# Alternating the layers of two token groups, with the norms and the sample group moved inside the stages and the weights packed on the host

## The chip, the cores and the metric

The kernel runs on all 8 cores of one Trainium2 chip (two dies of four cores). Every core does the same work on its own data. The metric is the device time of the slowest core, in microseconds (us), taken as the median of several runs. Some runs here fall in a slower state, in which some cores show a lower granted TensorE clock; such runs are named as slow and are left out of every comparison.

The engines are PE (TensorE, matrix products), ACT (ScalarE), DVE (VectorE), POOL (GpSimd) and SP (SyncE, which here only issues transfers). The lines of the profile use these names.

## The reference

The reference is one step of a two-layer trunk for a prompt (8 sequences of 2048 tokens, 1024 features, one sequence for each core) and for 128 sample rows (16 for each core). One layer is:

```python
h = rmsnorm(x, norm_g)                                  # over 1024 features
a_in, a_gate, u, v, b_gate = split(h @ w_in)            # w_in 1024 x 2560: five blocks of 512
# A: trailing means over 2, 4, 8, 16 positions (one window per 128 channels), minus the token
a_out = (pooled(a_in) @ w_pool) * pool_scale * silu(a_gate)
# B: chunks of 128 positions, 4 heads
b_out = u * (tril(w_s) @ rmsnorm(v) + b_s) * silu(b_gate)
x = x + concat(a_out, b_out) @ w_out                    # w_out 1024 x 1024
```

A sample row is one new token, so its trailing means also need up to 15 earlier rows of `a_in`, which come in as a state (`st`, two layers x 16 rows x 15 x 512). A final RMSNorm ends both paths. The weights arrive in float32 and are multiplied in bfloat16.

## The kernel before

The prompt is cut into four groups of 512 tokens. I call one group's pass through one layer a **stage**: norm, transposes, five projection blocks (V, A, two gates, U), pooling, chunk product, output projection, residual add. There are eight stages. The kernel before takes them group by group, (0,0), (0,1), (1,0) and so on, written as (group, layer):

```python
WIN_ORDER = (C_V, C_AIN, C_AGATE, C_BGATE, C_U)
for l in range(2):
    for cb in WIN_ORDER:                     # POOL's queue casts float32 to bfloat16 on the way
        wlist.append((win[l][:, :, cb:cb + 512],
                      win_d[l][:, cb:cb + 512].rearrange("(k p) e -> p k e", p=128), f"win{l}_{cb}"))
    # [cut: wpool and two halves of w_out]
issue_weights(100)                           # all of them at the start

for G in range(NG):                          # [cut: arguments and hooks]
    layer_group(G, 0, ...)                   # the second layer's norms run at the end of this stage
    layer_group(G, 1, ...)                   # the next group's norms run at the end of this one
fin_b = finals_batched(NG - 1, split=True)
sample_rest(1, mid_hook=fin_b)               # the sample group's second layer: at the very end
sample_final()
```

The sample group runs beside and after the last prompt stage, with 16 of the 128 rows of a matmul's output in use.

All work is emitted into one list for each engine and runs there **in that order**.

Of the kernel before, what the change touches and what calls it, by code (L numbers as in the profile page):

```python
# [28 lines left out]
NT = SEQ // 128  # L29
NHB = 3  # L30
HALO = 16
AW = HALO + GT
C_AIN, C_AGATE, C_U, C_V, C_BGATE = 0, 512, 1024, 1536, 2048
WINDOWS = (2, 4, 8, 16)

# [8 lines left out]

class Buf:
    __slots__ = ("name", "writer", "readers")

    def __init__(self, name):
        self.name = name
        self.writer = None  # L50
        self.readers = []

class Op:
    __slots__ = ("eng", "fn", "deps", "dma", "tok", "used", "group")

    def __init__(self, eng, fn, dma=None, group=False):
        self.eng = eng
        self.fn = fn
        self.deps = []
        self.dma = dma  # L60
        self.group = group
        self.tok = None
        self.used = False

class Sched:
    def __init__(self):
        self.ops = {e: [] for e in ENGS}
        self.all = []

    def emit(self, eng, fn, reads=(), writes=(), deps=(), dma=None, group=False):  # L70
        op = Op(eng, fn, dma, group)
# [3 lines left out]
        for b in reads:  # L75
            if b.writer is not None:
                dd.append(b.writer)
        for b in writes:
            dd.extend(b.readers)
            if b.writer is not None:  # L80
                dd.append(b.writer)
        dd.extend(d for d in deps if d is not None)
# [11 lines left out]
        for b in writes:  # L94
            b.writer = op
            b.readers = []
        self.ops[eng].append(op)
        self.all.append(op)
        return op

    def resolve(self):
        keys = {}
        dma_cnt = {}
        group_ops = {}
        for e in ENGS:
            cnt = 0
            for op in self.ops[e]:
                if op.dma is not None:
                    dma_cnt[op.dma] = dma_cnt.get(op.dma, 0) + 16
                    op.tok = (op.dma, dma_cnt[op.dma])  # L110
                    keys[op.dma] = None
                    if op.group:
                        group_ops.setdefault(op.dma, []).append(op)
                elif op.used:
                    cnt += 1
                    op.tok = (e, cnt)
                    keys[e] = None
        for k, ops in group_ops.items():
            for op in ops:
                op.tok = (k, dma_cnt[k])  # L120
        return keys

    def run_engine(self, e, h, sems):
        waited = {}
        for op in self.ops[e]:
            for d in op.deps:
                key, val = d.tok
                if waited.get(key, 0) < val:
                    h.wait_ge(sems[key], val)
                    waited[key] = val  # L130
# [5 lines left out]

class Banks:
    def __init__(self, tensors, tag):
        self.t = tensors
        self.bufs = [Buf(f"{tag}{i}") for i in range(len(tensors))]  # L140
        self.nxt = 0

    def alloc(self):
        i = self.nxt
        self.nxt = (self.nxt + 1) % len(self.t)
        return self.t[i], self.bufs[i]

def build_program():
# [12 lines left out]
    ng_d = din("norm_g", [2, D])  # L161
    win_d = din("w_in", [2, D, DIN])
    wpool_d = din("w_pool", [2, 4, 128, 128])
    psc_d = din("pool_scale", [2, WA])
    vng_d = din("v_norm_g", [2, WB])
    ws_d = din("w_s", [2, 4, 128, 128])
    bs_d = din("b_s", [2, 4, 128])
    wout_d = din("w_out", [2, D, D])
    fng_d = din("fng", [1, D])
    cid_d = din("c_ident", [128, 128])  # L170
    ctril_d = din("c_tril", [128, 128])
    cinv_d = din("c_invcnt", [1, 64])
    csel_d = din("c_sel", [120, 128])
    cm01_d = din("c_m01", [2, 2])
    gT_d = din("gT_h", [128, 16])
    pscT_d = din("pscT_h", [128, 8])
    ws00_d = din("ws00_h", [1, 8])
    bs0_d = din("bs0_h", [1, 8])
# [3 lines left out]
    pp_d = dout("pp", [2, PB, WA])  # L182
# [4 lines left out]
    with ExitStack() as es:  # L187
# [3 lines left out]
        def ps(name, shape, dt):  # L191
            return es.enter_context(nc.psum_tensor(name, list(shape), dt))

        win = [sb(f"win{l}", [128, 8, DIN], BF16) for l in range(2)]
        wout = [sb(f"wout{l}", [128, 8, D], BF16) for l in range(2)]
# [5 lines left out]
        a_sb = sb("a_sb", [128, 2, AW], F32)  # L201
        halo = sb("halo", [128, 2, 4, HALO], F32)
        Tt = sb("Tt", [128, 2, AW], F32)
        d_sb = sb("d_sb", [128, 4, GT], BF16)
        sg = sb("sg", [128, 4, GT], BF16)
        mix = sb("mix", [128, 8, GT], BF16)
        vn_sb = sb("vn_sb", [128, TPG, WB], BF16)
        vscr = sb("vscr", [128, WB], F32)
        junk = vscr[:, :].bitcast(BF16)
        vnf = sb("vnf", [128, WB], F32)  # L210
        pp_sb_ = vnf
        pp_sb = pp_sb_
        g_bc = sb("g_bc", [128, D], F32)
        gT = sb("gT", [128, 2, 8], F32)
        vg_bc = sb("vg_bc", [128, 2, WB], F32)
        psc = sb("psc", [128, 2, 4, 1], F32)
        ident = sb("ident", [128, 128], BF16)
        identf = xg[:, 5, 512:640]
        tril = xg[:, 5, 640:768]
        wsm = xg[:, 5, 768:1024].bitcast(BF16).rearrange("p (h j) -> p h j", h=4)  # L220
        invcnt = sb("invcnt", [128, 4, 16], F32)
        fix_t = sb("fix_t", [128, 16], F32)
        nhalf = sb("nhalf", [128, 4], F32)
        epsb = sb("epsb", [128, 1], F32)
        ones2 = sb("ones2", [2, 128], BF16)
        fl = lambda ap: ap.rearrange("p a b -> p (a b)")
        r3 = lambda ap: ap.rearrange("p (h i) -> p h i", h=4)
        bsf_l = [r3(xg[0:2, 4, 0:512]), r3(xg[0:2, 4, 512:1024])]
        bhif = r3(Tt[0:2, 0, 0:512])
        bhi = r3(hb[0:2, 2, 0:512])  # L230
        blo = r3(hb[0:2, 2, 512:1024])
        bias2 = sb("bias2", [2, 2, 4, 128], BF16)
        m01 = sb("m01", [2, 2], F32)
        ssx = sb("ssx", [128, 4 * 2 * SEQ // 128 // 2 + 64], F32)
        rsx = ssx
        ss4 = sb("ss4", [128, 2 * (SEQ // 128) + 4, 4], F32)
        rs4 = ss4
        xs_sb = xg[0:NS, 0, :]
        hbs = hb[0:NS, 0, :]
        hTs = sb("hTs", [128, 8, NS], BF16)  # L240
        st_sb = xg[0:120, 1, :].rearrange("p (t c) -> p t c", t=2)
        sel = sb("sel", [120, 2, 4, NS], F32)
        ains = pp_sb_[0:NS, :]
        ds_s = d_sb[0:NS, 0, :]
        dsT = sb("dsT", [128, 4, NS], BF16)
        tmp_s = Tt[0:NS, 0, 0:512]
        sga_s = a_sb[0:NS, 0, 0:512]
        sgb_s = a_sb[0:NS, 1, 0:512]
        s_s = Tt[0:NS, 1, 0:512]
        vns = vnf[0:NS, :]  # L250
        mixs = hb[0:NS, 1, :]
        mixTs = hTs
        psc_bc = vscr[0:NS, :]
        ws00 = sb("ws00", [NS, 2, 4, 1], F32)
        bs0 = sb("bs0", [NS, 2, 4, 1], F32)
# [8 lines left out]
        ALIAS = {  # L264
            "bhif": ["T0"], "bhi": ["hb2"], "blo": ["hb2"], "mixTs": ["hTs"], "pp_sb": ["vnf"],
            "hbs": ["hb0"], "st_sb0": ["x1"], "st_sb1": ["x1"], "ains": ["pp_sb"], "ds_s": ["d0"],
            "tmp_s": ["T0"], "sga_s": ["a_sb0", "a_halo0"], "sgb_s": ["a_sb1", "a_halo1"], "s_s": ["T1"],
            "vns": ["vnf"], "mixs": ["hb1"], "xs": ["x0"], "psc_bc": ["vscr"],
        }

        def buf(name):
            if name in ALIAS:
                return [buf(n) for n in ALIAS[name]]
# [4 lines left out]
        col_ctr = [0]  # L278

        def newcol():  # L280
            c = col_ctr[0]
            col_ctr[0] += 1
            return c
# [3 lines left out]
        def _okey():  # L287
            okey_ctr[0] += 1
            return f"out{okey_ctr[0]}"

        col4_ctr = [0]

        def newcol4():
            c = col4_ctr[0]
            col4_ctr[0] += 1
            return c

        stage_ops = []

        def cdma(out_ap, in_ap, wbuf, eng=SP):  # L300
            return S.emit(eng, lambda h, o=out_ap, i=in_ap: h.dma_start(out=o, in_=i),
                          writes=[wbuf], dma="const", group=True)

        def load_tile(t, deps=()):
            slot = t % NSLOT
            r0 = t * 128
            return S.emit(SP, lambda h, s=slot, r=r0: h.dma_start(out=xg[:, s, :], in_=x_d[r:r + 128, :]),
                          writes=[buf(f"x{slot}")], dma=f"xl{slot}", deps=deps)

        S.emit(SP, lambda h: h.dma_start(out=identf[:, :], in_=cid_d[:, :]), writes=[buf("identf")], dma="cident")  # L310
        for l in range(2):
            S.emit(SP, lambda h, l=l: h.dma_start(out=gT[:, l, :], in_=gT_d[:, l * 8:(l + 1) * 8]),
                   writes=[buf(f"gT{l}")], dma=f"cgT{l}")
        for t in range(4):
            load_tile(t)
        def prep_dma(l):
            stage_ops.append(S.emit(SP, lambda h, l=l: h.dma_start(
                out=bsf_l[l][:, :, :], in_=bs_d[l].rearrange("(o h) i -> o h i", o=1).broadcast_to([2, 4, 128])),
                writes=[buf(f"bsf{l}")], dma=f"bsf{l}"))

        ckey = [0]

        def cdma1(out_ap, in_ap, wbuf):
            ckey[0] += 1
            return S.emit(SP, lambda h, o=out_ap, i=in_ap: h.dma_start(out=o, in_=i), writes=[wbuf], dma=f"c{ckey[0]}")

# [758 lines left out]
```

## Time and profile before

The time before is 592.83 us (median of 3 runs, 591.86 to 595.3). The trace's slowest core spans 592.6 us.

| Part of the span | us | What limits it |
|---|---|---|
| First two of eight stages | 192 | weights arriving, work on DVE; PE busy 127 |
| A pair of stages after that | 116.3 | PE, busy 109.7 |
| After the last prompt matmul | 26 | a serial chain for the 16 sample rows |

The rows are read from the lines below. These lines are from the page of the kernel before: busy time and instructions of PE; then PE's busy share, the granted clock and the DMA engines' busy share in 40 equal slices of 14.8 us (9 is 90% or more); then packets, megabytes and share of the software queue that carries the weights.

```profile
PE 493.6 (83%) x2456; PEld 224.1 (38%) x2456; DVE 332.1 (56%) x748; ACT 175.4 (30%) x278; POOL 110.9 (19%) x158
PE   0259179868699999899999988999999989799993
PEclk9999778979989999999899999998999899988998
DMA  7999999940000000410000005100000021401003
q0 software_dynamic: 15616, 14.94, 18.8%
```

The reader sees three parts. The DMA engines are nearly full in the first eight slices, and PE has holes there. In the middle PE is nearly full. The next lines are from the table of engine busy time for chosen stretches (stretch, its length, busy time and instructions of PE, PEld, DVE, ACT and POOL, then granted clock, DMA share and GB/s).

```profile
0.00:192.00 192.00, 126.84 (x602) 56.91 (x603) 99.26 (x259) 48.71 (x74) 34.53 (x51) 0.91 0.70 110
192.00:308.50 116.50, 109.64 (x561) 50.68 (x560) 69.00 (x143) 40.59 (x64) 24.03 (x34) 0.99 0.10 37
308.50:424.60 116.10, 109.67 (x562) 50.65 (x560) 69.02 (x143) 40.60 (x64) 23.96 (x34) 0.99 0.10 37
```

The first two stages take 192 us. After that a pair of stages takes 116.3 us, of which PE is busy 109.7: PE is the limit. The end is different again. Lines of the timeline of PE (start, length, line and operation, output and inputs, count, and in brackets the idle time before it and what ended it):

```profile
562.25 3.63 PE L702 MATMUL pF<-wout,mix 128*128 128x512 bf16 x16
569.28 7.07 PE L759 MATMUL pF<-win,hTs 128*16 128x512 bf16 x32
580.57 5.30 PE L878 MATMUL pF<-wout,hTs 128*16 128x512 bf16 x16 [0.48 <-DVE hTs L750]
```

L702 is the prompt's last output projection. It is over at about 566 us, and 26 us of sample work follow. The sample's matmuls (`128*16`: 16 output columns of the array in use) cost as much as full ones (`128*128`): 32 in 7.07 us, and the 32 full ones from 191.77 us on took 7.07 us too.

### The profile page before, as it was taken

Reading aid. Unit: us, or ns where it says so; the run is one execution under the profiler, and the core shown is the slowest. Engines: PE = TensorE matmul, PEld = TensorE weight load, DVE = VectorE, ACT = ScalarE, POOL = GpSimd, SP = SyncE. Lnnn points to the kernel's source line nnn. Section 1 sums busy time; section 2 is a strip of 40 time slices with the busy share of each in tenths; the row PEclk is TensorE's granted clock in tenths of the full one; section 3 lists DMA queues with packets and bytes.
Section 4 is the critical chain, followed back from the end, with each engine's and each line's share of the span. In section 5 each row is a group of like instructions: output and inputs, shape, how many; then the busy total and the mean of one; then the engine's idle time right before and its main releaser. Section 6 shows DMA issues by size and latency. Waiting matters only on the chain.

```text
span 592.6 us, 7987 instructions; the slowest of 8 cores (582.6 to 592.6 us)
## 1 busy us (share of the span) xinstructions
PE 493.6 (83%) x2456; PEld 224.1 (38%) x2456; DVE 332.1 (56%) x748; ACT 175.4 (30%) x278; POOL 110.9 (19%) x158
## 2 busy tenths in 40 slices
PE   0259179868699999899999988999999989799993
PEld 0224023423235444344354434444544344334341
DVE  0247674448735664666357655673575456644556
ACT  2501040511223243433233425243234152211230
POOL 9002110113001501241005021501140215100020
PEclk9999778979989999999899999998999899988998
DMA  7999999940000000410000005100000021401003
GB/s 153 180 171 167 152 223 150 156 67 1 1 0 2 0 1 2 177 71 38 1 1 0 2 0 213 48 26 1 1 19 3 0 108 38 120 1 39 1 7 146
DMA packets 24244, 36.86 MB, mean 62 GB/s; under 512 B 3057, under 2 KB 18793, under 8 KB 24171
## 3 DMA queue, kind: packets, MB, share of 16 engines
q0 software_dynamic: 15616, 14.94, 18.8%
q1 hardware_dynamic: 8587, 21.42, 11.0%
q8 instruction: 20, 0.33, 0.2%
q14 instruction: 21, 0.17, 0.1%
HBM read 42.12 MB, written 10.09 MB: 88 GB/s over the span
## 4 chain that ended last, share of the span: by engine, by line
PE 54%; DVE 19%; issue 7%; DMA 6%; ACT 5%; POOL 4%; SPq 1%; another core or an unknown queue 1%; DVEq 1%; POOLq 0%; ACTq 0%
PE pF L506 23%; PE pF L702 16%; PE pF L519 9%; DMA xg<-w_s 4%; DVE win L376 3%; DVE Tt L543 3%; DVE mix L690 2%; DVE vn_sb L581 2%; ACT vscr L454 2%; DVE ss L569 2%; PE pF L759 2%; PE pT L487 2%; PE pF L878 2%; POOL Tt L543 1%; ACT hb L477 1%
## 5 line engine op out<-in xcount | busy, mean ns | idle before, releaser
L506 PE MATMUL pF<-hT,win 128*128 128x512 bf16 x1024 | 233.5, 385 | 10.4 <-ACT a_sb L642 4.6
L506 PEld LDWEIGHTS pF<-hT,win 128*128 128x128 bf16 x1024 | 100.8, 99 | 136.8 <-issue 21.4
L702 PE MATMUL pF<-wout,mix 128*128 128x512 bf16 x512 | 122.8, 397 | 7.3 <-DVE ssx L465 3.1
L702 PEld LDWEIGHTS pF<-wout,mix 128*128 128x128 bf16 x512 | 50.4, 101 | 68.6 <-issue 19.2
L519 PE MATMUL pF<-win,hT 128*128 128x512 bf16 x272 | 65.1, 397 | 10.5 <-DVE win L376 6.8
L468 POOL TENSOR_TENSOR ssx<-ssx,nhalf 128x1 f32<-128x1 f32 (+1 forms) x31 | 20.0, 646 | 227.9 <-DVE ssx L465 227.9
L707 DVE TENSOR_TENSOR xg<-pF,xg 128x512 f32<-128x512 f32 x64 | 44.1, 689 | 32.7 <-PE pF L702 31.3
L454 ACT ACTIVATE vscr<-xg 128x1024 bf16<-128x1024 f32 (+1 forms) x35 | 36.7, 1049 | 85.0 <-DVE xg L707 58.9
L477 ACT ACTIVATE hb<-xg,ssx 128x1024 bf16<-128x1024 f32 x32 | 36.7, 1148 | 60.6 <-POOL ssx L468 59.1
L575 POOL TENSOR_TENSOR ss<-ss,nhalf 128x4 f32<-128x4 f32 x32 | 32.4, 1012 | 106.5 <-DVE ss L573 106.5
L672 DVE TENSOR_TENSOR sg<-pF,sg 128x512 bf16<-128x512 f32 x32 | 22.1, 691 | 49.9 <-PE pF L506 36.3
L487 PE MATMUL pT<-ident,hb 128*128 128x128 bf16 x256 | 21.1, 230 | 31.4 <-ACT hb L477 31.4
L519 PEld LDWEIGHTS pF<-win,hT 128*128 128x128 bf16 x272 | 27.0, 102 | 43.9 <-issue 16.9
L642 ACT COPY a_sb<-pF 128x512 f32<-128x512 f32 x32 | 18.7, 585 | 83.2 <-DVE d_sb L560 32.6
L565 ACT ACTIVATE vscr<-pF 128x512 f32<-128x512 f32 x32 | 19.1, 595 | 81.4 <-PE pF L519 45.5
L552 DVE SCALAR_TENSOR_TENSOR d_sb<-Tt,a_sb 128x512 bf16<-128x512 f32 x32 | 22.1, 691 | 23.0 <-POOL halo L550 22.7
L581 DVE SCALAR_TENSOR_TENSOR vn_sb<-pF,ss,vg_bc 128x128 bf16<-128x128 f32 x120 | 33.8, 344 | 1.0 <-issue 0.4
L668 ACT ACTIVATE sg<-pF 128x512 bf16<-128x512 f32 x32 | 19.1, 597 | 49.1 <-DVE mix L662 25.7
L465 DVE TENSOR_SCALAR ssx<-ssx 128x1 f32<-128x1 f32 (+1 forms) x31 | 4.7, 152 | 50.4 <-ACT vscr L454 50.4
L487 PEld LDWEIGHTS pT<-ident,hb 128*128 128x128 bf16 x256 | 17.4, 103 | 40.5 <-issue 35.8
L491 DVE COPY hT<-pT 128x1024 bf16<-128x1024 bf16 x32 | 21.9, 687 | 17.1 <-PE pT L487 17.1
L543 DVE TENSOR_TENSOR Tt<-Tt 128x512 f32<-128x512 f32 (+3 forms) x40 | 27.9, 697 | 4.5 <-DVE Tt L543 0.5
(90 smaller groups left out, 386.2 us busy)
## 6 DMA issues: line engine op xcount, KB each, us to landing
win<-w_in POOLq DMA_DIRECT2D x10, 1024.0 KB, 67.3
xg<-x SPq DMA_DIRECT2D x16, 512.0 KB, 5.8
y<-xg SPq DMA_DIRECT2D x16, 512.0 KB, 2.9
wout<-w_out POOLq DMA_DIRECT2D x4, 1024.0 KB, 88.7
xg<-st SPq DMA_DIRECT2D x4, 240.0 KB, 2.7
pso<-st SPq DMA_DIRECT2D x2, 448.0 KB, 5.9
vg_bc<-v_norm_g SPq DMA_DIRECT2D x2, 256.0 KB, 18.0
xg<-w_s SPq DMA_DIRECT2D x2, 256.0 KB, 24.7
```

Source lines behind the costliest of these rows:

```text
L454: S.emit(ACT, lambda h: h.activation(out=junk[0:nparts, 0:n_feat], in_=src_ap, func=AF.Square, accum_out=ssx[0:nparts, c:c + 1]), reads=li ...
L477: S.emit(ACT, lambda h: h.activation(out=hb[:, j, :], in_=xa, func=AF.Copy, scale=rsx[:, c:c + 1]), reads=[xbuf(G, i), rb], writes=[buf(f" ...
L487: r = h.transpose(out=pt[:, k * 128:(k + 1) * 128], in_=hb[:, j, k * 128:(k + 1) * 128], identity=ident[:, :])
L506: r = h.matmul(out=pf[:, 0:GT], lhsT=win[l][:, k, col0:col0 + 128], rhs=hT[:, k, :], start=(k == 0), stop=(k == 7))
L519: r = h.matmul(out=pf[:, :], lhsT=hT[:, k, i * 128:(i + 1) * 128], rhs=win[l][:, k, col0:col0 + 512], start=(k == 0), stop=(k == 7))
L543: S.emit(PENG, lambda h, dst=dst, src=src, c0=c_from, sh=shift: h.tensor_tensor(out=dst[:, c0:AW], in0=src[:, c0:AW], in1=src[:, c0 - sh:A ...
L552: S.emit(DVE, lambda h, src=src: h.scalar_tensor_tensor(out=d_sb[:, g, :], in0=src[:, HALO:AW], scalar=1.0 / w, in1=a_sb[:, sl, HALO:AW], ...
L575: S.emit(POOL, lambda h: h.tensor_tensor(out=rs4[:, c, :], in0=rs4[:, c, :], in1=nhalf[:, :], op=ALU.pow), reads=[rb, buf("nhalf")], write ...
L581: r = h.scalar_tensor_tensor(out=o, in0=pf[:, hh * 128:(hh + 1) * 128], scalar=rs4[:, c, hh:hh + 1], in1=vg_bc[:, l, hh * 128:(hh + 1) * 1 ...
L672: S.emit(DVE, lambda h, pf=pf, hh=hh: h.tensor_tensor(out=sg[:, hh, :], in0=pf[:, 0:GT], in1=sg[:, hh, :], op=ALU.mult), reads=[pfb, buf(f ...
L702: r = h.matmul(out=pf[:, :], lhsT=mix[:, k, i * 128:(i + 1) * 128], rhs=wout[l][:, k, hf * 512:(hf + 1) * 512], start=(k == 0), stop=(k == 7))
L707: S.emit(DVE, lambda h, pf=pf, xa=xa, hf=hf: h.tensor_tensor(out=xa[:, hf * 512:(hf + 1) * 512], in0=pf[:, :], in1=xa[:, hf * 512:(hf + 1) ...
```

## The change

Its intent is to give each layer's weights twice as long to arrive (two groups run through layer 0 before layer 1 is needed), to keep PE from waiting between stages, to take work off PE and DVE, and to take the sample group off the end. The core of the diff, with cuts marked:

```diff
-for G in range(NG): layer_group(G, 0, ...); layer_group(G, 1, ...)
+order = [(0, 0), (1, 0), (0, 1), (1, 1), (2, 0), (3, 0), (2, 1), (3, 1)]
+hooks = {
+    (0, 0): {"g0": [prep_ws], "g1": [lambda: load_state(0), lambda: load_state(1)], "b0": [load_w],
+             "b2": [load_w], "u0": [load_w], "u2": [load_w], "o00": [misc_loads],
+             "o11": [lambda: state_sum(0), lambda: state_sum(1)], "o30": [load_w]},
+    (1, 0): {"v2": [load_w], "a0": [load_w]},
+    (2, 0): {"v0": [lambda: sample_layer(0, lambda: None)]},
+    (2, 1): {"v0": [lambda: sample_layer(1, sample_final)]},
+}
 # hooks: "g0" is "after the first unit of the first gate", "b" the second gate,
 # "o11" after the second half of the second tile of the output projection

 # in stage(): the next stage's norms run inside this one
+unit_u(G, l, hh); norm_b(*nxt, hh); norm_c(*nxt, hh)        # [cut: conditions]
+norm_tr(*nxt, 0); norm_tr(*nxt, 1)                          # before the output projection
+# [cut] norm_tr(*nxt, 2) after tile 0 of it, norm_tr(*nxt, 3) after tile 1

 # weights: each block is one contiguous 16 KB row per partition, packed on the host
-win_d[l][:, cb:cb + 512].rearrange("(k p) e -> p k e", p=128)
+win_d = din("win_h", [2, 5, 128, 8 * 512])
 # norm gain: out of the weights, into the eviction of the transposes
-h.tensor_scalar(out=win[l][:, k, cb:cb + 512], ..., scalar1=gT[:, l, k:k + 1], op0=ALU.mult)   # x80
+S.emit(DVE, lambda h: h.tensor_tensor(out=hT[:, :, i * 128:(i + 1) * 128], in0=pt[...],
+    in1=gT(l).unsqueeze(2).broadcast_to([128, 8, 128]), op=ALU.mult), ...)
 # chunk bias: from a matmul into DVE's eviction; wide windows: shifted adds -> one scan [cut]

 # sample group: four column quadrants, output partitions 32j..32j+31
-h.matmul(out=pf[0:NS, :], lhsT=hTs[:, k, :], rhs=win[l][:, k, col0:col0 + 512], ...)
+h.matmul(out=p1_[32 * j:32 * j + 32, :]..., lhsT=hTs[:, k, :],
+         rhs=win[l][:, 0:4, k, j * 128:(j + 1) * 128], ..., tile_position=(0, 32 * j))

 # all on SP's queue, in this order
+gate = [buf(f"win0_{U_}").writer]                           # x of group 1 waits for the U block
+for i in range(TPG): load_x(1, i, deps=gate)
+sdma(qc[:, :], q_d[:, :], writes=[buf("qc")])
+for j in range(4):                                          # four pieces of 16 KB, one buffer
+    sdma(xs[32 * j:32 * j + NS, :], xs_d[:, j * 256:(j + 1) * 256], writes=[buf("xs")], key=f"xs{j}")
+# [cut] pso: state rows to the output; then load_state(0), load_state(1), four pieces each
+def state_sum(l):                                           # DVE: sums of 1, 3, 7, 15 state rows
+    for j in range(4):
+        S.emit(DVE, lambda h, j=j, n=n: h.tensor_reduce(out=ssum[32 * j:32 * j + NS, l, :], ...))
```

## The prediction

> What bounds the kernel now. The per-stretch table of engine busy time splits the slowest core's 592.6 us into three parts.
> (a) Start, 0 to 192 us, for two of the eight stages (4 token groups x 2 layers). The DMA engines are saturated until about 122 us. The timeline shows layer-0 projection blocks landing at about 23 (first), 55 and 61.5 us (last), and the last layer-1 output weights at about 127 us: some 7 us per 2.1 MB block, about 295 GB/s of reads. Added to that: 80 norm-gain multiplications of weights on DVE (21.5 us in the groups), mask and bias preparation, an idle PE at 60 to 74 us (its clock granted falls to 0.5), and in the second stage a wait of pooling and v-norm on each other (PE busy 74% at 140-150, 62% at 150-160).
> (b) Steady state: one group, both layers, takes 116.3 us, PE busy 109.7, clock 0.99; 512-column matmuls start every 0.216 us. PE is the limit; waits and transposes cost about 7 us per pair.
> (c) End: 533 to 592 us, last output projection with the sample group on 16 of 128 rows. Its full-width matmuls are 112 x 0.216 = 24 us, and after the last prompt matmul (566 us) 26 us of serial sample chain follow.
>
> What the change does. Two groups alternate, so layer 0 runs twice (about 54 us more) before layer-1 weights are needed, and the next stage's norms run under the present one's gate and U matmuls; the transposes sit where PE would wait for the mix. The gain moves to the transpose eviction: 80 multiplications go, but 32 evictions grow from 0.69 to about 1.2 us (DVE about +16 us spread out, harmless at about 60% busy). The bias matmul goes: 32 x 0.32 = 10 us of PE. Pooling of wide windows becomes a scan, estimated 1.2 us each instead of 2 to 2.8. Blocks of 16 KB per partition help DMA a little; I estimate 6.5 to 7 us per block.
>
> Sum.
> - Stage 1 follows the weights: first block about 18 us, U about 46, output weights about 70 (x of group 1 competes). Then 12 to 14 us of output projection: stage ends at about 85.
> - Seven stages at (116.3 - 7)/2 - 1.3 = 53.3 us: 373.
> - [...]
> - Remaining bubbles 5; tail (last add, square sum, scale, store) 8.
> Total 483, so 484 us, range 465 to 515. Nearly all of the saving (about 105 start, 25 to 30 steady, most of 26 at the end[...]) is on the critical path, because PE is the limit throughout.
>
> Chances: faster 0.97, same 0.02, slower 0.01.
>
> Right if: stage 2 starts at 75 to 95 us; stages 2 to 8 take 52 to 56 us each with PE idle under 2 us; no PE gap over 5 us after 90 us; tail under 12 us. Wrong if: output weights land after 85 us; a stage takes over 57 us because DVE or POOL (U products wait for a POOL multiplication, 1.04 us each) falls behind; quadrant matmuls run one after another[...].
>
> [...] Before, all eight cores show 0.99 in the steady stretches[...].

The sum came to 483 us. The terms still printed add up to 471 (85, 373, 5 and 8); the missing one, 12 us for the sample group, is cut, and so are the 10 us for serial quadrant matmuls.

## The result

The kernel after takes 521.57 us (median of 4 runs: 520.88, 521.4, 521.74 and one slow run of 533.28; the median of the three fast ones is 521.4), beside 592.52 for the kernel before on the same chip. The ratio is 0.8786 (95% interval 0.8755 to 0.8817). Ratios here are the mean time of one kernel's fast runs over that of the other's in the same rounds, so they are not quite the ratio of the medians. The kernel is 12% faster, and 6.6 us slower than the top of the predicted range.

The page of the kernel after (slices of 13 us), with the same lines as above, and the shares of the chain that ended last, by engine:

```profile
PE 456.0 (88%) x2486; PEld 214.1 (41%) x2486; DVE 284.8 (55%) x484; ACT 168.2 (32%) x276; POOL 156.6 (30%) x224
PE   8795767740699999999999999999999999999994
PEclk9899697785699999999999999999999999999997
DMA  6999999534490000005500350000200000030003
q0 software_dynamic: 2160, 14.94, 17.6%
PE 66%; DMA 21%; DVE 4%; issue 4%; ACT 2%; POOL 1%; SPq 1%; POOLq 0%; DVEq 0%; ACTq 0%
```

From the twelfth slice PE is full to the end. The loss is all in the first eleven slices: one of them is empty (0), and 21% of the last chain is DMA. The packing shows too: the software queue carries the same megabytes in 2160 packets instead of 15616, so a packet is 6.9 KB instead of 957 B (14.94 MB over the count). The steady part, in the table of stretches:

```profile
186.70:239.90 53.20, 52.44 (x278) 24.93 (x277) 33.29 (x61) 21.38 (x34) 17.37 (x26) 1.00 0.03 12
293.00:350.40 57.40, 56.63 (x384) 27.38 (x383) 35.41 (x64) 20.83 (x38) 19.62 (x27) 1.00 0.21 66
```

A plain stage takes 53.2 us with PE idle for 0.8; a stage with the sample group in it takes 57.4. The largest waits of PE (what waited, for what, microseconds, times, longest):

```profile
PE pF L418 <- DVE xg L567: 25.4, 1, 25.4
PE pT L388 <- ACT hb L378: 17.6, 19, 4.0
PE pF L523 <- DMA wpool<-wpool_h: 8.9, 1, 8.9
```

The first is one single wait, and all eight cores have it (22.9 to 26.8 us). PE's V projection of stage 2 needs a PSUM bank that DVE's residual add (L567) has yet to empty. DVE had nothing hard to do. The chain of waits over this stretch, in order of time (start, length, what; cut to the long pieces):

```profile
56.70 44.37 DMA xs_sb<-xs
101.13 1.63 DMA xs_sb<-xs
102.83 1.71 DMA xs_sb<-xs
...
106.32 5.82 DMA win<-st
...
123.36 4.23 DMA wout<-st
...
130.50 3.37 DVE ssum L885
```

This is read from top to bottom as one sentence. The first 16 KB of sample input took 44.37 us to land. That is not the price of 16 KB alone: on SP's queue it stood behind group 1's x (four tiles of 512 KB, the last landed at 92 us) and `qc` (386 KB, landed 43.7 us after its issue at 56.15), 2450 KB in all. The pieces behind it were issued one after the other; then came the state, piece by piece; then DVE could sum it. DVE's own timeline shows where it stood meanwhile:

```profile
119.37 6.17 DVE L885 TENSOR_REDUCE ssum<-win 16x128 f32<-16x128 f32 x4 [20.74 <-DMA win<-st]
127.68 6.17 DVE L885 TENSOR_REDUCE ssum<-wout 16x128 f32<-16x128 f32 x4 [1.74 <-DMA wout<-st]
134.16 2.88 DVE L567 TENSOR_TENSOR xg<-pF,xg 128x512 f32<-128x512 f32 x4
```

DVE sat idle for 20.74 us at the head of its queue, and the four residual adds that PE needed stood behind the sums. They ran in the order of DVE's list, and the price here is 25.4 us.

The second loss is the length of stage 1. The output weights landed at about 72 us (70 predicted), but the output projection ended only at 106. The transposes of group 1 are now part of stage 1, and its x arrived late. ACT's timeline for the last of four tiles:

```profile
92.06 1.06 ACT L354 ACTIVATE hb<-xg 128x1024 bf16<-128x1024 f32 x1 [4.47 <-DMA xg<-x]
```

That tile's x landed at 92 us. PE transposed it at about 96 us, ahead of the last 32 matmuls of the projection (9.6 us), and the stage ended at 106.

The sum can now be set beside the prediction's. All measured numbers are read from the profiled core's trace.

| Term | Predicted, us | Measured, us |
|---|---|---|
| Stage 1 ends | 85 | 106.0 |
| Stages 2 to 8 without sample and without the one long wait | 373 | 372.3 |
| Sample group | 12 | 8.8 (57.4 + 57.6 less twice 53.1) |
| Bubbles; measured: the one long wait | 5 | 25.4 |
| Tail | 8 | 7.5 |
| Sum | 483 | 520.0 |

Two terms are wrong, by 21 and by 20 us. The experiments ask what causes each of them.

### The profile page after: what moved, and what is told of

Same layout as the page of the kernel before. It is cut to its first block, busy times and chain, and to the rows that moved or that the text cites. A ratio compares the mean times of both kernels' runs of the same rounds, so it can differ in the third digit from the quotient of the medians.

```text
span 520.1 us, 7837 instructions; the slowest of 8 cores (509.4 to 520.1 us)
## 1 busy us (share of the span) xinstructions
PE 456.0 (88%) x2486; PEld 214.1 (41%) x2486; DVE 284.8 (55%) x484; ACT 168.2 (32%) x276; POOL 156.6 (30%) x224
## 3 DMA queue, kind: packets, MB, share of 16 engines
q0 software_dynamic: 2160, 14.94, 17.6%
## 4 chain that ended last, share of the span: by engine, by line
PE 66%; DMA 21%; DVE 4%; issue 4%; ACT 2%; POOL 1%; SPq 1%; POOLq 0%; DVEq 0%; ACTq 0%
PE pF L406 37%; PE pF L562 15%; DMA xs_sb<-xs 9%; PE pF L418 9%; DMA win<-win_h 6%; DMA wout<-st 2%; DMA win<-st 2%; DMA xg<-x 2%; ACT hb L378 1%; PE pT L388 1%; PE pF L536 1%; DVE hT L392 1%; PE pF L523 1%; SPq L292 1%; DVE ssum L885 1%
## 5 line engine op out<-in xcount | busy, mean ns | idle before, releaser
L418 PE MATMUL pF<-win,hT 128*128 128x512 bf16 x256 | 59.1, 388 | 25.4 <-DVE xg L567 25.4
L562 PEld LDWEIGHTS pF<-wout,mix 128*128 128x128 bf16 x512 | 50.3, 100 | 59.9 <-issue 7.1
L354 ACT ACTIVATE hb<-xg 128x1024 bf16<-128x1024 f32 x48 | 50.3, 1049 | 60.6 <-DVE xg L567 37.8
L545 POOL TENSOR_TENSOR mix<-vscr,mix 128x512 bf16<-128x512 f32 x32 | 36.4, 1156 | 99.3 <-DVE vscr L541 99.2
L362 POOL TENSOR_TENSOR rsx<-rsx,nhalf 128x1 f32<-128x1 f32 x48 | 26.4, 553 | 122.0 <-DVE rsx L359 122.0
L517 ACT ACTIVATE mix<-pF 128x512 bf16<-128x512 f32 x64 | 38.2, 597 | 76.1 <-PE pF L406 73.5
L434 POOL TENSOR_TENSOR rs<-rs,nhalf 128x4 f32<-128x4 f32 x32 | 35.2, 1101 | 72.2 <-DVE rs L432 72.1
L567 DVE TENSOR_TENSOR xg<-pF,xg 128x512 f32<-128x512 f32 x64 | 44.0, 690 | 21.3 <-PE pF L562 19.2
L378 ACT ACTIVATE hb<-xg,rsx 128x1024 bf16<-128x1024 f32 x32 | 36.1, 1144 | 55.5 <-POOL rsx L362 55.4
L541 DVE SCALAR_TENSOR_TENSOR vscr<-pF,kc,bias 128x512 f32<-128x512 f32 x32 | 23.3, 749 | 45.6 <-PE pF L536 35.3
L392 DVE TENSOR_TENSOR hT<-pT,kc 128x1024 bf16<-128x1024 bf16 x32 | 38.4, 1217 | 2.5 <-PE pT L388 2.4
L501 DVE SCALAR_TENSOR_TENSOR mix<-Tt,a_sb 128x512 bf16<-128x512 f32 x32 | 22.2, 693 | 24.3 <-POOL halo L493 21.5
L429 DVE TENSOR_REDUCE ss<-vscr 128x4 f32<-128x512 f32 x32 | 21.9, 683 | 13.5 <-ACT vscr L425 13.2
```

The costliest lines, as they stand in the source:

```text
L354: S.emit(ACT, lambda h: h.activation(out=junk, in_=src, func=AF.Square, accum_out=ssx[:, c:c + 1]), reads=[srcb], writes=[junkb, buf(f"ssx ...
L362: S.emit(POOL, lambda h: h.tensor_tensor(out=rsx[:, c:c + 1], in0=rsx[:, c:c + 1], in1=nhalf[:, 0:1], op=ALU.pow), reads=[buf(f"rsx{c}"), ...
L378: S.emit(ACT, lambda h: h.activation(out=hb[:, j, :], in_=xap(G, i), func=AF.Copy, scale=rsx[:, c:c + 1]), reads=[xbuf(G, i), buf(f"rsx{c} ...
L392: S.emit(DVE, lambda h: h.tensor_tensor(out=hT[:, :, i * 128:(i + 1) * 128], in0=pt[:, :].rearrange("p (k t) -> p k t", k=8), in1=gT(l).un ...
L418: r = h.matmul(out=pf[:, :], lhsT=hT[:, k, i * 128:(i + 1) * 128], rhs=win[l][:, V_, k, :], start=(k == 0), stop=(k == 7))
L434: S.emit(POOL, lambda h: h.tensor_tensor(out=rs4[:, c, :], in0=rs4[:, c, :], in1=nhalf[:, :], op=ALU.pow), reads=[rb, buf("nhalf")], write ...
```

## The experiments

Fourteen kernels ran, and all gave correct results. The letters in the expectations name theories. A: DVE is held by the state sums. C: the layer-1 weights, issued in stage 1 though nothing needs them before stage 3, crowd out x, the sample input and the state. E: the long packets of the packed weights crowd out the small transfers. G: only the order and the chaining on SP's queue delay the state. I, J, L and P belong to single later runs and are explained there. Times are medians; ratios are against the kernel before in the same rounds.

### Four single edits of the kernel after

**e1_sum_late.** The sums move to stage 2. The layer-1 loads whose space the state uses move behind them.

```diff
 (0, 0): ... "o00": [misc_loads],
-        "o11": [lambda: state_sum(0), lambda: state_sum(1)], "o30": [load_w]},
-(1, 0): {"v2": [load_w], "a0": [load_w]},
+(1, 0): {"a3": [lambda: state_sum(0)], "b0": [lambda: state_sum(1)], "u2": [load_w], "o00": [load_w], "o30": [load_w]},
```

> Edit: the two sums of the sample state on DVE (12.3 us of work plus the wait for their loads) move from the output projection of stage 1 into stage 2 (behind the last pooling unit and the first B gate unit); the last three layer-1 weight loads follow them; no transfer of stage 1 moves. Theory A (the 25.4 us PE gap at 109.6 us is DVE held in program order by a sum whose input lands at 119 us): the gap shrinks to under 6 us and the kernel takes 495 to 502 us. Rival B (PE would have waited there anyway, for weights or for x of group 1): the gap stays over 15 us and the time stays above 512 us.

Measured: 499.38 us (498.56 to 500.02), ratio 0.8422 (0.8392 to 0.8452). The wait of 25.4 us is gone from PE's list, whose largest single waits are now:

```profile
PE pF L523 <- DMA wpool<-wpool_h: 8.2, 1, 8.2
PE pF L523 <- DVE mix L501: 4.9, 1, 4.9
```

The state's pieces landed hardly earlier (SP's chain of them ran from 104.7 to 120.6 us); only DVE no longer stood waiting for them. This shows theory A. Of the wait's 25.4 us the kernel gained 22.2. The 12.3 us of summing now stand in stage 2, which takes 59.9 us on the profiled core; PE's 4.9 us are a wait for an instruction of DVE that stands right behind the first sum.

**e2_l1_late.** The order on DVE stays as it was, but all layer-1 weights are issued in stage 2.

```diff
-(0, 0): ... "b0": [load_w], "b2": [load_w], "u0": [load_w], "u2": [load_w], ... "o30": [load_w]
-(1, 0): {"v2": [load_w], "a0": [load_w]},
+(1, 0): {"v0": [load_w], "v1": [load_w], "v2": [load_w], "v3": [load_w], "a0": [load_w], "a1": [load_w], "a2": [load_w]},
```

> Edit: the layer-1 weight loads, four of which are issued during stage 1, are all issued in stage 2; nothing else moves. Theory C (transfers on the SP queue are slow because layer-1 weights, not needed before 187 us, share the DMA engines): x of group 1 lands by about 74 us instead of 92, the sample rows within 25 us of issue instead of 44, the state by 90 us; stage 1 ends about 10 us earlier and the gap falls to about 5 us: 487 to 497 us. Rival D (the SP queue is slow by itself, by its chain of waits or by layer-0 weights alone): x lands within 4 us of before, and the time changes by under 8 us.

Measured: 496.67 us (496.5 to 497.17), ratio 0.8376. Group 1's x had landed by about 75 us instead of 92 (its second tile at 72), and the first piece of sample input took 18.6 us instead of 44.4. Stage 2 started at 92.15 us on the profiled core instead of 105.97. The wait on DVE shrank but did not vanish (expected about 5 us, measured 14.1). A line of PE's waits, and one of DVE's timeline:

```profile
PE pF L418 <- DVE xg L567: 14.1, 1, 14.1
```

```profile
93.59 6.20 DVE L885 TENSOR_REDUCE ssum<-win 16x128 f32<-16x128 f32 x4 [6.48 <-DMA win<-st]
```

So theory C explains most of the late end of stage 1 and a little under half of the wait in stage 2 (11.3 of 25.4 us).

**e3_unpacked.** The weights are read from their original layout, in rows of 2 KB, and nothing else is changed.

```diff
-wq.append((win[l][:, blk, :, :].rearrange("p k e -> p (k e)"), win_d[l][blk], ...))
+wq.append((win[l][:, blk, :, :], win_d[l][:, COLS[blk]:COLS[blk] + 512].rearrange("(k p) e -> p k e", p=128), ...))
```

> Edit: weight blocks are read from the original row layout as before the change (2 KB runs instead of 16 KB per partition); the program is otherwise the same. Theory E (long packets of the packed weights take the DMA engines away from the SP queue): x of group 1 and the sample rows land 10 us or more earlier, weights a little later, and the time falls by 5 to 15 us. Rival F (packing speeds the weights up and costs the SP queue nothing): the last layer-0 projection block lands 3 to 8 us later than 54 us and the time rises by 3 to 10 us.

Measured: 516.1 us (515.62 to 519.82), ratio 0.8719 (0.8677 to 0.8761). By the medians it is 5.5 us faster than the kernel after, which ran on another chip; the intervals of the two ratios just overlap (0.8755 and 0.8761). The trace supports theory E more clearly than the time does. The U block landed at the same 54.1 us, but the first piece of sample input, behind the same 2434 KB of x and `qc`, took 16.7 us instead of 44.4, ACT no longer waited for group 1's x, and stage 2 began at 91.45 us. The DMA view shows what changed hands. First the kernel after from 56 to 92 us, then e3 from 56 to 73 us (packets, megabytes, share; q0 carries the weights, q1 is SP's queue):

```profile
q0 software_dynamic: 659, 4.78, 80.0%
q1 hardware_dynamic: 606, 2.19, 21.5%
```

```profile
q0 software_dynamic: 1319, 1.33, 58.6%
q1 hardware_dynamic: 751, 2.51, 47.1%
```

With long weight packets SP's queue got less than a third of the bytes, with short ones nearly two thirds. The weights paid for it: the last output weights landed at 78 us instead of 72. Then the state's chain was slow in its turn, while the layer-1 weights still streamed. Lines of SP's timeline, of DVE's timeline and of PE's waits:

```profile
87.22 23.13 SPq L292 DMA_DIRECT2D win<-st  x4
```

```profile
113.13 6.17 DVE L885 TENSOR_REDUCE ssum<-win 16x128 f32<-16x128 f32 x4 [26.72 <-DMA win<-st]
```

```profile
PE pF L418 <- DVE xg L567: 34.2, 1, 34.2
```

Of the 14.5 us gained in stage 1 (91.45 against 105.97), 8.8 were lost in a longer wait in stage 2 (34.2 against 25.4), because DVE was still bound to the end of the same chain.

**e4_sp_order.** The state is loaded right behind group 1's x, and the pieces no longer wait for each other.

```diff
+load_state(0); load_state(1)                                # ahead of qc and xs
-writes=[b_(f"st{l}")], key=f"st{l}{j}")
+writes=[b_(f"st{l}")] if j == 3 else [], key=f"st{l}")     # the same for xs
-"g1": [lambda: load_state(0), lambda: load_state(1)],
```

> Edit: the state loads are issued right behind x of group 1 and, like the four loads of the sample rows, no longer wait for one another. Theory G (the chain of waits on the SP queue makes the state late): the state lands by about 75 us, the gap falls to under 8 us, 498 to 505 us. Rival C (the DMA engines are full until about 100 us, so what is issued earlier still lands at about 95 to 100 us): the gap falls only to 12 to 17 us, 507 to 514 us.

Measured: 503.75 us (502.79 to 504.99), ratio 0.8498. The time is what theory G expected, and the wait in stage 2, 10.3 us, lies between the two. The state was issued at 55 to 60 us, and DVE waited for it until 101.75: some 40 us, and not by 75 us as theory G had it, but where rival C put it. Chaining and order therefore cost some 18 us, and they are not the whole: the state now stood behind group 1's x on SP's queue, and that x landed at about 91 us beside the stream of weights.

### Both causes removed, and what showed next

**e5_late_both** issues the layer-1 weights in stage 2 and spreads the sums over stage 2 (three short ones at one hook, the long one at the next).

```diff
+(1, 0): {"v0": [load_w], ..., "v3": [load_w], "b0": [lambda: state_sum(0, (0, 1, 2))], "u3": [lambda: state_sum(0, (3,))],
+         "o10": [load_w], "o20": [lambda: state_sum(1, (0, 1, 2))], "o31": [lambda: state_sum(1, (3,))]},
+(0, 1): {"v1": [load_w, load_w]},
```

> Edit: both earlier cures together: layer-1 weights are issued in stage 2, the state sums run in stage 2, now in four pieces spread over it. Theory (late x of group 1 costs stage 1 some 14 us, the state wait costs stage 2 some 25 us, and the two are separate): stage 2 starts at about 91 us as in the run with late layer-1 loads, has no gap over 2 us, and the kernel takes 479 to 485 us. Rival (they are one and the same delay, either cure takes most of it): 492 to 497 us.

Measured: the two fast runs took 487.97 and 489.82 us, ratio 0.8228 (0.8191 to 0.8264); two more were slow (508.7 and 511.16). Removing both takes away about 33 us (0.8786 - 0.8228 of 593), more than e1 or e2 alone (22.2 and 24.9) and less than their sum, since each of them also shortens the wait that the other removes. The miss of about 5 us against the expectation has a visible part: the long sum of 3.44 us at hook "u3" stood ahead of the small norm instructions, and the transposes waited 4.2 us for them.

**e6_wpool** also moves the small pooling weights ahead of the last two projection blocks, since the kernel after waits 8.9 us for them.

```diff
-wq.append((wpool..., "wpool"))
+wq.insert(3, (wpool..., "wpool"))
```

> Edit on top of the former: the pooling map's weights are loaded behind the third projection block instead of behind the fifth. Theory H (PE waits 9 us at 47 us for these 0.5 MB, which stand behind a block that it needs only later): the B gate units run at 48 to 55 us, U ends at about 63 instead of 75 us, stage 1 ends 4 to 7 us earlier: 474 to 480 us. Rival I (stage 1 is bound by the arrival of the output weights and of x, so PE only waits elsewhere): within 2 us of the former run.

Measured: fast runs 492.4 to 492.96 us, ratio 0.8295 (0.8262 to 0.8327), about 4 us slower than e5 (the intervals all but part). The wait for `wpool` is gone and another has come, longer than it was:

```profile
PE pF L406 <- ACT mix L517: 11.7, 1, 11.7
```

This is the rival, I, though it expected no loss. ACT, in order, had reached the first norm instruction of group 1 earlier. That x landed at about 70 us (ACT waited 13.5 us for it), and the gates that PE needed stood behind it. Taking one wait away only moved the engine to the next thing that was late.

**e7_x1_free** adds to e6 that group 1's x no longer waits for the U block (theory J: the gate, meant to protect the weights, costs more than it saves).

```diff
-load_x(1, i, deps=gate)
+load_x(1, i)
```

> Edit on top of the former: x of group 1 no longer waits for the last projection block to land, so it is issued at about 47 instead of 54 us. Theory J (x of group 1 is the last thing that stage 1 waits for): 2 to 4 us faster than the former. Rival K (the DMA engines are full, so the bytes only change places and the last projection block comes later): within 1.5 us, or slower.

Measured: fast runs 486.2 to 488.11 us, ratio 0.8199 (0.8171 to 0.8228), about 5.5 us faster than e6 and more than theory J's 2 to 4. The wait on ACT vanished; PE now waits 3.7 us for output weights and 4.2 us for a projection block, both really on their way.

**e8_v_first** issues the first two weight blocks at the very start, ahead of x.

```diff
+load_w(); load_w()
-if i == 0: load_w(deps=[x_ops[2]])
-else: load_w()
```

> Edit on top of the former: the first two projection blocks are issued at the start, beside x of group 0, instead of after three tiles of x have landed (12.9 us). Theory L (the DMA engines have idle time in the first 13 us and are the limit from there to the end of stage 1): the last projection block lands 4 to 7 us earlier, and the kernel is 4 to 7 us faster than the former, 468 to 475 us. Rival M (x of group 0 now lands later and PE starts later by as much): within 2 us or slower.

Measured: 510.55 us (509.8 to 511.05), with a lowered clock in all four runs, so no ratio of fast runs is to be had. In the profiled run cores 2, 3, 6 and 7 had it, two in each die. The table of stretches for core 3 and then for core 0 of the same run (the last but two numbers are the granted clock):

```profile
160.00:210.00 50.00, 49.93 (x227) 22.32 (x225) 26.53 (x47) 18.56 (x29) 13.40 (x22) 0.81 0.25 46
310.00:360.00 50.00, 48.72 (x288) 23.39 (x286) 29.10 (x50) 16.86 (x26) 17.09 (x23) 1.00 0.08 12
```

```profile
160.00:210.00 50.00, 48.35 (x258) 22.94 (x257) 33.16 (x60) 21.14 (x34) 16.59 (x25) 1.00 0.35 80
```

Core 3 runs at 0.81 of the clock from about 144 to 304 us and at full speed afterwards; core 0 was never slowed. The undisturbed cores span 481.2 to 483.3 us, so the edit itself is about neutral or slightly faster, and the gain of 4 to 7 us that theory L expected does not show. Whether it caused the lower clock is open: other kernels of that chip had slow runs too.

### The last step: what SP's queue waits for

The next four ran on one chip in five rounds, without a slow run. e9 is e7 with the sums, and the three weight loads that must follow them, at other hooks; e10 to e12 each change one thing in it.

**e9_sums_spread**

```diff
 # e7 with
+(1, 0): {"v0": [load_w], ..., "v3": [load_w], "g0": [lambda: state_sum(0, (0, 1, 2))], "g2": [lambda: state_sum(0, (3,))],
+         "b0": [load_w], "b1": [lambda: state_sum(1, (0, 1, 2))], "o20": [lambda: state_sum(1, (3,))], "o31": [load_w, load_w]},
```

> Edit against the kernel with free x of group 1: only the places of the four pieces of the state sums in stage 2 change, away from the stretch in which DVE must release the next stage's norms. Theory N (the 3.4 us sum behind the last U product held up the norm of the third tile, and PE waited 4.3 us for it): stage 2 takes 53 to 55 us instead of 59.8, fast runs at 480 to 484 us against 487. Rival (DVE work anywhere in stage 2 costs the same): within 2 us. [...]

Measured: 492.78 us (490.07 to 495.49), ratio 0.8328, worse than expected. One line of PE's waits and one of SP's timeline tell why:

```profile
PE pF L406 <- DVE vscr L541: 10.0, 1, 10.0
```

```profile
88.96 24.02 SPq L292 DMA_DIRECT2D wout<-st  x4
```

Issuing layer 1's state, the end of the serial chain, took 24.02 us, because the layer-1 weights were issued from 90.37 us on and now streamed beside it. (e7 has the same chain, 26.56 us, but its sums stood later.) DVE stood in its list at the sum, and PE behind DVE. It is the first fault of the kernel after, in stage 2 instead of stage 1.

**e10_v_after_x0** starts the first weight block behind one x tile, not three (theory L: 2 to 4 us).

```diff
-load_w(deps=[x_ops[2]])
+load_w(deps=[x_ops[0]])
```

> Edit on top of the former: the first projection block waits for the first tile of x instead of the third (about 7 instead of 12.9 us). Theory L (the DMA engines are the limit of stage 1 and idle in part before 13 us): 2 to 4 us faster in fast runs, 477 to 481 us. Rival M (later tiles of x land later and PE starts later): within 1.5 us. [...]

Measured: 489.63 us (489.36 to 491.87), ratio 0.8284 (0.8257 to 0.8312) against e9's 0.8328 (0.8298 to 0.8359). The medians differ by 3.2 us, but the intervals overlap, and in the two traces stage 3 starts no earlier (table below; e9's profiled run was its fastest). It stays unclear, and the expected 477 to 481 us were missed.

**e11_unpacked_late** is e9 with the original layout of the weights, as in e3.

> Edit against the kernel with spread sums: weights read in the original row layout (2 KB runs) instead of packed by the host. Theory O (packing gave no bandwidth, and with layer-1 weights out of the way its harm to the SP queue is small too): within 2 us. Rival E (long packets still take the engines from x of group 1): 3 to 6 us faster. Rival F (short packets are slower once nothing else competes): the last projection block lands 3 or more us later and the time rises by 3 us or more.

Measured: 485.11 us (484.41 to 485.68), ratio 0.8197 (0.8171 to 0.8222): clearly faster than e9, by 7.7 us. The chain that took 24.02 us takes

```profile
88.10 7.34 SPq L292 DMA_DIRECT2D wout<-st  x4
```

and the sum's wait is gone. On the other side, PE waited 9.4 us in all for projection blocks, and stage 2 started about 4 us later than in e9. That delay is itself a cause, because the layer-1 weights are issued at the start of stage 2. POOL's timeline of e9 and then of e11, first layer-1 weight:

```profile
90.37 0.65 POOL L292 DMA_DIRECT2D win<-win_h  x1
```

```profile
96.68 0.99 POOL L292 DMA_DIRECT2D win<-w_in  x1
```

In e11 all four pieces had been issued before the weights were, so nothing streamed beside the chain but for its last piece. The packed e6, whose layer-1 weights came at 100.45 us, has a short chain too (8.53 us from 91.95). So the 7.7 us are real, but this pair does not show that long packets delay the state: the chain was short wherever the weights came after it.

**e12_no_warm** is e9 without the warm-up matmuls that keep PE busy before the first weights land (theory P: they buy nothing that matters here).

```diff
-warm_up(30)
-warm_up(8)
```

> Edit against the kernel with spread sums: the 62 warm-up matmuls on zeros before and between the first transposes are left out. Theory P (stage 1 is bound by transfers, so a cold PE in the first block costs nothing at its end): within 1.5 us. Rival: [...]the first block takes 3 to 7 us longer, 2 us or more in the end. [...]

Measured: 492.21 us (490.57 to 494.68), within 0.6 us of e9. The first V block took 9.01 us instead of 7.07, but that does not show in the time.

**e13_all_packed** is e10 with e4's edit: the state is loaded right behind group 1's x, before any layer-1 weight, and no piece waits for another. **e14_all_unpacked** is the same with the original layout. This pair asks whether packing hurts by itself or only through the queue that waited.

> Edit on top of the run where the first block waits for one tile of x: the state loads are issued right behind x of group 1 and, like the sample rows, no longer wait for one another; so they are ahead of the layer-1 weights. Theory Q (the wait for the state is made of the chain and of what streams while it is paid; with both out of the way nothing of it is left): no PE wait over 4 us in stage 2, stage 3 starts at about 140 us instead of 154, fast runs at 475 to 481 us. Rival (long packets alone delay the state): a wait of 5 us or more stays in stage 2, above 484 us. [...]

> Edit on top of the former: weights in the original row layout (2 KB runs). If nothing waits on the SP queue any more, packing does not matter: within 2 us of the former (theory Q). If packets of x of group 1 are still held up by the packed stream, 2 to 5 us faster; if packing does carry more bytes per us, 2 to 5 us slower.

Measured, in five rounds on one chip without slow runs: e13 takes 481.69 us (480.76 to 482.94), ratio 0.8134 (0.8106 to 0.8163). e14 takes 488.07 us (486.06 to 489.01), ratio 0.8237 (0.8203 to 0.827). The order has turned round: packed is now faster by 6.4 us. e13 beats both given kernels. Of theory Q's signs, no PE wait over 4 us is left in stage 2, but stage 3 starts at 143.8 us (table below) and not at 140, and the time is just above the expected 475 to 481. SP's timeline of e13, and PE's two lines of waits for weights, all of layer 0:

```profile
47.03 2.33 SPq L292 DMA_DIRECT2D win<-st  x4
49.41 2.35 SPq L292 DMA_DIRECT2D wout<-st  x4
```

```profile
PE pF L562 <- DMA wout<-wout_h: 7.3, 1, 7.3
PE pF L406 <- DMA win<-win_h: 3.5, 2, 2.3
```

The state's pieces still take 24 to 27 us to land in e13 (10 to 14 in e14), but they are issued at 47 us and needed after 100, so nothing waits for them. What remains are waits for layer-0 weights themselves.

The start of a stage differs by some microseconds from core to core, so this table gives means of all eight cores of each profiled run, read from the timelines of PE. The time follows the slowest core: in e9 the cores start stage 3 between 140.7 and 154.8 us, in e11 between 145.9 and 149.2.

| Kernel | Stage 2 starts, us | Stage 3 starts, us | Time, us |
|---|---|---|---|
| after | 102.2 | 182.7 | 521.57 |
| e1, sums in stage 2 | 101.5 | 162.0 | 499.38 |
| e2, layer-1 weights in stage 2 | 90.6 | 159.4 | 496.67 |
| e9, both and more | 85.8 | 149.0 | 492.78 |
| e10, first block earlier | 86.0 | 150.9 | 489.63 |
| e11, e9 unpacked | 89.9 | 147.5 | 485.11 |
| e13, all, packed | 87.0 | 143.8 | 481.69 |
| e14, all, unpacked | 92.2 | 150.4 | 488.07 |

Between e13 and e14, 5.2 of the 6.6 us to stage 3 are in stage 1, where packed blocks arrive sooner (on the profiled cores the U matmuls begin at 57.2 us in e13 and at 62.0 in e14), and 1.4 in stage 2. As in e3, the layout decides who goes first: by the landing events of the traces (means of the cores) the last output weights of layer 0 landed at 71.9 us in e13 and 76.7 in e14, group 1's x at 69.8 and 59.8. In this order of work PE waits for the weights and no longer for x. From stage 3 on the two traces agree: stages of 53.1 to 57.6 us in both.

## Why the prediction was wrong

The direction was right, and so was most of the sum. The time missed the range because two terms were mis-sized. A third smaller error went the other way.

1. **"Stage 1 follows the weights ... stage ends at about 85" failed by 21 us.** The weights kept the schedule roughly: the first block landed at 24 instead of 18 us, U at 54 instead of 46, and the last output weights at about 72 instead of 70. But the step assumed that the stage follows the weights alone. The prediction named group 1's x as a competitor and gave it no time. The change had put that group's norms and transposes into stage 1, so x became an input of stage 1, issued only when U had landed and itself landing at 92 us. What held it back were weights that no one needed: with layer 1's loads moved to stage 2 (e2), x landed by 75 us, and stage 2 started 11.6 us earlier (mean of the cores). e3 brought x as early, by 71 us, with these loads in place and only their layout changed; so the delay needed both, the early stream and its long packets. With x also freed from its gate and the pooling weights moved forward, e9 starts stage 2 at 85.8 and e13 at 87.0, close to the 85 predicted.

2. **"Remaining bubbles 5" failed by 20 us.** The prediction costed the sample group's matmuls but not its data. The state sums sat in DVE's list in front of residual adds that PE needs, and their data sat at the end of a serial chain on SP's queue, behind 2450 KB of x, `qc` and sample input that took 44.4 us to land. Moving the sums (e1) took away 22.2 us with the chain as late as before. So the wait was DVE's order; the lateness of the chain set its size. The sums' own work is dear for its size as well: on 16 partitions, read with a stride, they cost 1.72 ns for each further element ((3360 - 274) ns over 1920 - 128 elements), while a contiguous sum of 512 elements on 128 partitions (L429) took 685 ns, at most 1.34 ns each. What makes the difference was not tested.

3. **"Blocks of 16 KB per partition help DMA a little" was incomplete.** The five projection blocks landed 7.4 us apart in both layouts (24.3 to 54.1 us in the kernel after, 24.7 to 54.1 in e3); 6.5 to 7 were predicted. What packing changed is the share of the two queues once x competed. In the kernel after that was probably a loss (e3: the original layout is 5.5 us faster by the medians, with intervals that overlap slightly). e11 is clearly faster than e9 (7.7 us), but there the layer-1 weights came too late to meet the state's chain. Packing is a gain of 6.4 us in e13 against e14, where no engine stands waiting for a small transfer.

4. **"Seven stages at ... 53.3 us: 373" was right:** 372.3. Part of the agreement is luck. The measured 372.3 includes 5.7 us of ordinary PE idle time (406.5 us from the start of stage 2 to the last matmul, less 375.4 of busy PE and the 25.4), which the prediction had put under bubbles; without it these stages take 366.6, and all the bubbles together are 31.1. The gain's move to the transpose eviction also cost what was expected (1217 ns each, predicted 1.2 us), so did the scans (1225 to 1278 ns, predicted 1.2 us), and POOL's multiplications end no wait of PE in the list of waits.

5. **The sample group's term, 12, was too high:** 8.8 us. It was the author's estimate, and no trace stood behind what it took the quadrants to save. The trace of the kernel after shows what the column quadrants bring:

```profile
307.25 1.91 PE L652 MATMUL pF<-win,hTs 128*32 128x512 bf16 x32
```

These 32 matmuls take 1.91 us, the 32 before took 7.07: 3.7 times faster for four tiles, in eight sets in a row.

6. **The tail, "8", was right** (7.5). **The main risk, a lower clock, did not come in the fast runs**: the profiled run of the kernel after shows 1.00 in the steady stages on all eight cores. A clock of 0.81 did come in e8, on cores 2, 3, 6 and 7, two in each die, for about 160 us; of the other slow runs only mean clocks are on record (0.91 to 0.93).

Of the signs that the prediction gave for itself, the start of stage 2 (75 to 95) and "no PE gap over 5 us after 90 us" came out against it; the plain stages after the second (52 to 56, idle under 2) and the tail came out for it. Its list of what would make it wrong named late output weights, POOL or DVE falling behind in a stage, and serial quadrant matmuls. None of these was the cause as it was meant: DVE was not overloaded when it held up stage 2, but idle for 20.74 us at a wait in its list.

What stays open: how much of the crowding out belongs to packet length and how much to the weights' place in time. e3 shows the first alone and e2 the second alone, but they were not crossed without the chain. It is also open why packets of 6.9 KB leave SP's queue so much less: where both had work, the two queues moved 659 and 606 packets in the kernel after, and 1319 and 751 in e3; no run tests this by itself. And what brings on the low clock in e8 is not known.

## What to carry to other kernels

When a change moves data or small reductions into the middle of a run, cost the place of their wait, not only their work: in the kernel after, 12.3 us of sums that waited for a chain of small transfers in DVE's list cost PE 25.4 us. Issue small transfers that someone will need early, unchained, and ahead of long weight streams (e13), and issue a stream no earlier than its use and the bandwidth require (e2). Judge a layout change such as packing only after that, because its sign turned from e9 and e11 (packed slower by 7.7 us) to e13 and e14 (packed faster by 6.4 us) with what else was on the queues at the time.
